# Conformer convolution: TensorE blocks in three of eight chunks, VectorE on two chunks in turn, the stage in one written order

## The chip, the core and the metric

The kernel runs on one core of a Trainium2 chip. A core has five engines that take their own instruction streams and wait for each other by semaphores: TensorE (PE in the profile, with its weight loads as PEld), VectorE (DVE), ScalarE (ACT), GpSimd (POOL) and SyncE (SP), which here only starts transfers. Matrix products go to PSUM, everything else lies in SBUF. The metric is the device time of one execution in microseconds; the time before is the median of three runs.

## The reference

A two-layer decoder trunk over 512 tokens with 1024 channels. Layer 0 has a recurrent and pooling mixer, layer 1 a conformer convolution; each layer goes on with cross-attention into 256 memory tokens and a gated MLP. The change lies in the conformer of layer 1:

```python
def conformer_conv(x, norm, w1, b1, dw_w, dw_b, ln_g, ln_b, w2, b2):
    h = rms_norm(x, norm) @ w1 + b1
    h = jax.nn.glu(h, axis=-1)
    h = causal_dwconv(h, dw_w, dw_b)
    h = jax.nn.silu(layer_norm(h, ln_g, ln_b))
    return h @ w2 + b2
```

`causal_dwconv` gives each of 1024 channels its own 31 taps over time: output t is the sum over s of tap s times the input at t - s, plus a bias. The cross-attention that follows needs keys and values of the memory, which do not depend on x: `k = (m @ wk)`, `v = (m @ wv)`.

## The kernel before

Activations lie as 8 chunks of 128 channels by 512 tokens, channels on the partitions. Every float32 operand of a product is split into a high part (rounded, written by ScalarE) and a low part (the difference, written by VectorE or GpSimd), and a product is three products, high-high, high-low and low-high: `mm3`, lines 183 to 185. A 1024 x 128 weight is one transfer into a `raw` buffer (three of them), split into `whi` and `wlo` (four of each).

The conformer is the function `conformer`, line 1342. Its steps for chunk c:

- Norm: `Scaled.scale` takes token sums on TensorE (L316), their root and reciprocal on ScalarE and VectorE (L323, L324), a diagonal (L326), and spreads it to all partitions on TensorE (L256). `split` scales x (L265) and makes its high (L173) and low half (L178).
- Projections: a gate half and a value half, `project` or `project_all`, each 24 products into a PSUM buffer named `mm`.
- Gating: ScalarE's sigmoid (L1349), then VectorE's `h = (value + bias) * sigmoid` (L1362).
- Convolution, three ways at once. *TensorE*: `conv_pe` (L1391) takes the first `4 * PE_GROUPS[c]` taps. Four transfers first make a stacked copy of h with four shifts (L1369), `spread` (L1381, GpSimd) lays taps on small diagonals, and a group of four taps is four 128 x 32 products. *ScalarE and GpSimd*: five taps, scaled copies (L1410, L1413) added up by GpSimd (L1414). *VectorE*: all others, one SCALAR_TENSOR_TENSOR a shift onto the PSUM accumulator (L1416).
- `merge` (L1425): accumulator plus bias plus GpSimd's sum. After chunks 3 and 7, `quarters` (L293) adds four chunks into the LayerNorm mean.

Before, TensorE takes 3, 2, 3, 2, 3, 3, 3 and 8 groups of the eight chunks. Chunk 7 leaves nothing to VectorE. The order of the main part is the scheduler's, from the order of the program and priorities; only the last part, from chunk 7's block on, is in written order for TensorE, ScalarE, VectorE and GpSimd (`tc.manual_schedule`). SyncE's order is the scheduler's throughout. Keys 0 to 3 of layer 1's attention (`mem.keys`, 24 products of 256 columns each) stand ahead of the norm's use, keys 4 to 7 further down. The value sums (`mem.sums`, L442) fill TensorE while the LayerNorm's chain runs.

Of the kernel before, what the change touches and what calls it, by code (L numbers as in the profile page):

```python
# [15 lines left out]
P = 128  # L16
T = 512
# [18 lines left out]
PE_GROUPS = [3, 2, 3, 2, 3, 3, 3, 8]  # L36
N_POOL = [5] * 7 + [0]
LAG = 5

KE = 4  # L40
# [6 lines left out]
    ("c_dw_w", (TAPS - 4 * min(PE_GROUPS)) * C), ("c_dw_b", C), ("c_ln_g", C), ("c_ln_b", C), ("c_b_pw2", C),  # L47
# [12 lines left out]
def trunk(ctx: ExitStack, tc: tile.TileContext, I: dict, out: list):  # L60
# [32 lines left out]
    def tmp_f(n=T):  # L93
        return tmp.tile([P, n], F32, tag="tmp", name=nm("tmp"))
# [139 lines left out]
    class Scaled:  # L234


        def __init__(self, gain):
            self.gain, self.x, self.ss = gain, [None] * C, None

        def feed(self, c):  # L240
            sq = tmp_f()
            A.activation(sq, X[c], AF.Square)
# [26 lines left out]
        def high(self, c):  # L269
            self.x[c] = self.x[c], high(self.x[c])  # L270
# [18 lines left out]
    def quarters(ps, xs):  # L289

        def quarter(j):
            n = len(xs) - 4 + j
            return PE.matmul(ps[32 * j : 32 * j + 32], onesf[:, :32], xs[n], start=n < 4, stop=n >= 4)  # L293


        with tc.issue_after(quarter(3).ins):
            for j in range(3):
                quarter(j)
# [500 lines left out]
    def ffn(layer, norm, nxt, seven):  # L799
# [267 lines left out]
        if nxt:  # L1067
            mem = Memory(1)
            mem.operand(0)
            mem.operand(1)  # L1070
            mem.outputs()
            parked = []
            for n in range(KE):
# [268 lines left out]
    def conformer(norm, nxt, mem, parked):  # L1342
# [4 lines left out]
        def gate(c, psb):  # L1347
            b = tmp_f()
            A.activation(b, psb, AF.Sigmoid, bias=col("c_b_pw1", C + c))  # L1349
            return b  # L1350

        def pieces(c):
            return load_w(I["pw1"][C + c], V if c == 2 else G), load_w(I["pw1"][c], G)

        def glu(c, w):
            b = gate(c, project(w[0], c, norm.x))
            gated(c, b, project(w[1], c, norm.x))

        def gated(c, b, psa):
            h = tmp.tile([P, T + 4], F32, tag="h", name=nm("h"), bufs=4)  # L1360
            G.memset(h[:, :4], 0.0)
            V.scalar_tensor_tensor(h[:, 4:], psa, col("c_b_pw1", c), b, op0=ALU.add, op1=ALU.mult)  # L1362
            stacked = [act_f() for _ in range(4)]
            for j in range(4):
# [5 lines left out]
            hs[c] = h[:, 4:], stacked  # L1370

# [13 lines left out]
        def conv_pe(c):  # L1385

            accs[c] = aux_ps()
# [7 lines left out]


            with tc.issue_after(tile(0, 3).ins):
                for g in range(PE_GROUPS[c]):
                    for j in range(3 if g == 0 else 4):
                        last = tile(g, j)  # L1400
            return last

        def conv(c):
            h, ps = hs[c][0], accs[c]
            z = act_f()
            first = 4 * PE_GROUPS[c]
            for s in range(first, first + N_POOL[c]):
                if s == first:
# [6 lines left out]
            for i, s in enumerate(range(first + N_POOL[c], TAPS)):  # L1415
                V.scalar_tensor_tensor(ps[:, s:], h[:, : T - s], tap(s, c), ps[:, s:], op0=ALU.mult, op1=ALU.add)  # L1416
                if i == LAG and pend:
                    merge(*pend.pop())
            if pend:
                merge(*pend.pop())  # L1420
            pend.append((c, z, ps))

        def merge(c, z, ps):
            if N_POOL[c]:
                V.scalar_tensor_tensor(z, ps, col("c_dw_b", c), z, op0=ALU.add, op1=ALU.add)  # L1425
            else:
                A.activation(z, ps, AF.Identity, bias=col("c_dw_b", c))
            outs.append(z)
            if c % 4 == 3:
                quarters(mu, outs)  # L1430

        pend, taps = [], [None] * C
        accs = [None] * C
        w = [load_w(I["pw1"][n]) for n in (C, 0, C + 1, 1)]
# [5 lines left out]
        spread(0)  # L1440
        spread(1)
        with tc.high_priority(URGENT):
            for c in range(C):
                norm.split(c)
        ps = project_all(w[:3], norm.x)
        gated(0, gate(0, ps[0]), ps[1])
        gated(1, gate(1, ps[2]), project(w[3], 1, norm.x))
        mu = stat_ps()
        w = pieces(2)
        for c in range(C - 1):  # L1450
            b = None
            if c == 0:
                b = gate(2, project(w[0], 2, norm.x))
            if c == 1:
                gated(2, gate2, project(w[1], 2, norm.x))
                w = pieces(3)
            elif c > 1:
                glu(c + 1, w)
                if c < C - 2:
                    w = pieces(c + 2)  # L1460
            gate2 = b
            if c in (0, C - 2):
                mem.keys(KE + c // 6)
            conv_pe(c)
            if c < C - 2:
                spread(c + 2)
            conv(c)
        xs = [None] * C
        with tc.manual_schedule(engines=ORDERED):
            w = [mem.key_piece(n) for n in (KE + 2, KE + 3)]  # L1470
            mem.eng = G
            ready = [mem.piece(i, park=True) for i in range(3)]
            for n in range(2):
                mem.keys(KE + 2 + n, w[n])
            ready.append(mem.piece(3, park=True))
            last = conv_pe(C - 1)
            ps = [[mm_ps(), mm_ps()] for _ in range(2)]
            z = act_f()
            A.activation(z, accs[C - 1], AF.Identity, bias=col("c_dw_b", C - 1))
            merge(*pend.pop())  # L1480
            outs.append(z)
            mem.eng = None
            ready += [mem.piece(i) for i in (4, 5)]
# [7 lines left out]
            quarters(mu, outs)  # L1491
# [6 lines left out]
            for c in range(C):  # L1498
# [3 lines left out]
                if c == 3:  # L1502
                    go(3)
                    quarters(var, sqs)
# [3 lines left out]
            quarters(var, sqs)  # L1508
# [214 lines left out]
def _layout(inputs):  # L1723
# [3 lines left out]
    a["c_dw_w"] = a["c_dw_w"][:, : TAPS - 4 * min(PE_GROUPS)]  # L1727
# [51 lines left out]
```

## Time and profile before

| | |
|---|---|
| runs | 1446.60, 1447.25, 1445.86 us; median 1446.6 |
| the profiled execution | 1445.47 us, of which the span is 1443.0 us |
| granted TensorE clock | 0.999 |
| TensorE busy | 1433.5 us, 99% of the span |
| VectorE, ScalarE, GpSimd busy | 81%, 55%, 19% |
| the stretch 774 to 871 us (convolution) | TensorE 97.0 of 97.0 us, VectorE 85.0, ScalarE 41.4, GpSimd 72.6 |

Times in the trace count from the start of the span. A row of the timeline has start, length, engine, line, operation and, in brackets, the idle time ahead of it and what ended that. TensorE's instructions are pipelined: the distance between starts says more than a length. In rows of groups, the count is behind the x, then busy time and mean ns of one, then idle time ahead. An instruction's line is that of the kernel it belongs to.

### The profile page before, as it was taken

Reading aid. Unit: us, or ns where it says so; the run is one execution under the profiler, and the core shown is the slowest. Engines: PE = TensorE matmul, PEld = TensorE weight load, DVE = VectorE, ACT = ScalarE, POOL = GpSimd, SP = SyncE. Lnnn points to the kernel's source line nnn. Section 1 sums busy time; section 2 is a strip of 40 time slices with the busy share of each in tenths; the row PEclk is TensorE's granted clock in tenths of the full one; section 3 lists DMA queues with packets and bytes.
Section 4 is the critical chain, followed back from the end, with each engine's and each line's share of the span. In section 5 each row is a group of like instructions: output and inputs, shape, how many; then the busy total and the mean of one; then the engine's idle time right before and its main releaser. Section 6 shows DMA issues by size and latency. Waiting matters only on the chain.

```text
span 1443.0 us, 22827 instructions
## 1 busy us (share of the span) xinstructions
PE 1433.5 (99%) x8608; PEld 1260.1 (87%) x8608; DVE 1162.5 (81%) x1916; ACT 787.3 (55%) x1305; POOL 274.8 (19%) x307
## 2 busy tenths in 40 slices
PE   9999999999999999999999999999999999999997
PEld 8888888988899999999887676899888999999997
DVE  6987775768788888888875897878788888888885
ACT  7668754657544444444545447666664444444433
POOL 0012300100022212212006841010001222221201
PEclk9999999999999999999999999999999999999999
DMA  8522232532567777876526654335245777777741
GB/s 303 190 88 89 89 130 73 125 96 88 161 151 166 185 157 166 181 168 146 158 88 177 165 155 151 112 81 138 90 124 128 173 183 159 168 182 163 160 126 59
DMA packets 80398, 205.33 MB, mean 142 GB/s; under 512 B 8992, under 2 KB 10272, under 8 KB 80288
## 3 DMA queue, kind: packets, MB, share of 16 engines
q1 hardware_dynamic: 53504, 155.36, 34.6%
q0 software_dynamic: 26496, 48.25, 20.4%
q8 instruction: 67, 1.10, 0.3%
q14 instruction: 43, 0.35, 0.1%
q10 hardware_dynamic: 288, 0.27, 0.1%
HBM read 145.13 MB, written 2.10 MB: 102 GB/s over the span
## 4 chain that ended last, share of the span: by engine, by line
PE 95%; DVE 2%; ACT 1%; DMA 1%; issue 0%; POOL 0%; SPq 0%; DVEq 0%; POOLq 0%; ACTq 0%
PE mm L183 23%; PE mm L184 23%; PE mm L185 23%; PE aux L183 7%; PE aux L184 7%; PE aux L185 7%; PE mm L442 3%; PE aux L1391 2%; PE aux L515 0%; DMA raw<-in_wv 0%; DVE wlo L164 0%; POOL tmp L1234 0%; DMA raw<-in_wdown 0%; ACT whi L163 0%; PE stat L316 0%
## 5 line engine op out<-in xcount | busy, mean ns | idle before, releaser
L183 PE MATMUL mm<-act,whi 128*128 128x512 f32 (+2 forms) x1093 | 385.3, 354 | 0.3 <-ACT act L849 0.3
L184 PE MATMUL mm<-act,whi 128*128 128x512 f32 (+2 forms) x1093 | 385.0, 352 | 0.1
L185 PE MATMUL mm<-act,wlo 128*128 128x512 f32 (+2 forms) x1093 | 384.7, 352 | 0.0
L183 PEld LDWEIGHTS mm<-act,whi 128*128 128x128 f32 x1093 | 206.3, 189 | 35.1 <-issue 3.3
L184 PEld LDWEIGHTS mm<-act,whi 128*128 128x128 f32 x1093 | 206.6, 189 | 29.4 <-DVE act L164 1.0
L185 PEld LDWEIGHTS mm<-act,wlo 128*128 128x128 f32 x1093 | 206.6, 189 | 27.1
L779 ACT ACTIVATE bigr<-raw 128x512 fp32r<-128x512 f32 x160 | 100.5, 629 | 158.5 <-DMA raw<-wa 67.8
L185 PE MATMUL mm<-bigr,bigr 128*128 128x256 f32 x640 | 181.1, 283 | 0.0
L184 PE MATMUL mm<-bigr,bigr 128*128 128x256 f32 x640 | 181.1, 283 | 0.0
L183 PE MATMUL mm<-bigr,bigr 128*128 128x256 f32 x640 | 180.9, 283 | 0.0
L168 DVE TENSOR_TENSOR tmp<-mm,tmp 128x256 f32<-128x256 f32 x322 | 130.9, 419 | 34.1 <-PE mm L185 27.8
L183 PE MATMUL aux<-act,whi 128*128 128x512 f32 x399 | 156.3, 392 | 0.0
L184 PE MATMUL aux<-act,whi 128*128 128x512 f32 x399 | 156.2, 392 | 0.0
L185 PE MATMUL aux<-act,wlo 128*128 128x512 f32 x399 | 155.2, 389 | 0.0
L163 ACT ACTIVATE whi<-raw 128x1024 fp32r<-128x1024 f32 (+1 forms) x95 | 96.2, 1019 | 96.7 <-PE mm L184 64.7
L786 DVE TENSOR_TENSOR bigr<-raw,bigr 128x512 fp32r<-128x512 f32 x160 | 109.9, 688 | 33.3 <-ACT bigr L779 31.2
L164 DVE TENSOR_TENSOR wlo<-raw,whi 128x1024 fp32r<-128x1024 f32 (+1 forms) x84 | 103.0, 1230 | 31.5 <-ACT whi L163 31.4
L184 PEld LDWEIGHTS mm<-bigr,bigr 128*128 128x128 f32 x640 | 122.7, 192 | 1.6
L183 PEld LDWEIGHTS mm<-bigr,bigr 128*128 128x128 f32 x640 | 122.7, 192 | 1.6
L185 PEld LDWEIGHTS mm<-bigr,bigr 128*128 128x128 f32 x640 | 122.7, 192 | 0.0
L789 POOL DMA_DIRECT2D raw<-raw x46 | 39.8, 866 | 359.3 <-DVE wlo L786 316.0
L793 POOL DMA_DIRECT2D raw<-wa x46 | 39.7, 864 | 302.4 <-DVE bigr L786 252.5
(338 smaller groups left out, 2958.4 us busy)
## 6 DMA issues: line engine op xcount, KB each, us to landing
raw<-wa POOLq DMA_DIRECT2D x138, 256.0 KB, 4.5
big<-in_wdown SPq DMA_DIRECT2D x42, 512.0 KB, 6.7
wa<-in_wpair SPq DMA_DIRECT2D x80, 256.0 KB, 3.4
raw<-in_wpair SPq DMA_DIRECT2D x40, 512.0 KB, 5.7
raw<-in_pw SPq DMA_DIRECT2D x24, 512.0 KB, 3.5
raw<-raw POOLq DMA_DIRECT2D x46, 256.0 KB, 7.5
raw<-in_win SPq DMA_DIRECT2D x20, 512.0 KB, 3.3
raw<-in_wk SPq DMA_DIRECT2D x16, 512.0 KB, 4.2
```

Source lines behind the costliest of these rows:

```text
L163: A.activation(hi, src, AF.Copy)
L164: fetched[1] = (eng or V).tensor_tensor(lo, src, hi.bitcast(F32), op=ALU.subtract)
L168: V.tensor_tensor(out, a, b, op=ALU.add)
L183: PE.matmul(ps, wh, xh, start=first, stop=False)
L184: PE.matmul(ps, wh, xl, start=False, stop=False)
L185: PE.matmul(ps, wl, xh, start=False, stop=last)
L442: PE.matmul(p, m[j], x, start=k == 0 and j == 0 and x is hi, stop=k == C - 1 and x is lo)
L779: A.activation(self.w[name][0], self.block(name), AF.Copy)
L786: V.tensor_tensor(lo, self.block(name), hi.bitcast(F32), op=ALU.subtract)
L789: G.dma_start(self.r, self.z, accum_op=ALU.add)
L793: G.dma_start(self.r, self.a22, accum_op=ALU.add)
L1391: return PE.matmul(accs[c][32 * j : 32 * j + 32, s:], taps[c][:, 4 * g + j], hs[c][1][j][:, : T - s], start=s == 0, stop=g == PE_GROUPS[c] ...
```

## The change

`PE_GROUPS` becomes 0, 0, 0, 6, 0, 5, 0, 6: TensorE blocks only in chunks 3, 5 and 7, 17 groups in place of 27. Their accumulators come from the `mm` buffers. A chunk without a block makes no stacked copies (12 transfers remain of 32); its accumulator starts with a TENSOR_SCALAR for shift 0 on VectorE, and ScalarE and GpSimd take shifts 1 to 5. All eight chunks now have five taps there. VectorE's shifts go from 106 to 140.

The whole stage from the first projections on is one written order for TensorE, ScalarE, VectorE, GpSimd and now SyncE. It is given as a script of short steps: G and V a gate and value projection, F the next load and the split of the next weight (with GpSimd for the low half), g and S sigmoid and gating, T shifts on VectorE, P taps on ScalarE and GpSimd, C a TensorE block, W its taps, M merge, K, k, l a key's products, high and low half, Q the LayerNorm sums. Steps T of two chunks stand in turn. Only keys 0 and 1 stay ahead of the norm (`KE` = 2; four keys' weights are still split ahead, `PARKED`). The norm's chunks are written as scaled(c + 1) ahead of low(c), and two one-element activations (`warm`) take ScalarE's table loads earlier: `token` (square root) and `gates` (sigmoid). The parameter block holds 31 taps a channel in place of 23.

TensorE at the norm, before. The last products of key 1, the spread, then key 2 (`mm_7771`):

```order
L183 MATMUL mm_7732<-bigr_7468,act_7514 128x256
L184 MATMUL mm_7732<-bigr_7469,act_7514 128x256
L185 MATMUL mm_7732<-bigr_7468,act_7515 128x256
L256 MATMUL aux_7769<-tmp_7767,unit 128x512
L183 MATMUL mm_7771<-bigr_7458,act_7526 128x256
L184 MATMUL mm_7771<-bigr_7459,act_7526 128x256
```

The same place now (lines are one or two higher; `mm_7738` is key 1, `mm_7832` the first gate projection):

```order
L184 MATMUL mm_7738<-bigr_7468,act_7514 128x256
L257 MATMUL aux_7775<-tmp_7773,unit 128x512
L185 MATMUL mm_7738<-bigr_7469,act_7514 128x256
```
```order
L184 MATMUL mm_7738<-bigr_7468,act_7514 128x256
L185 MATMUL mm_7738<-bigr_7469,act_7514 128x256
L186 MATMUL mm_7738<-bigr_7468,act_7515 128x256
L184 MATMUL mm_7832<-act_7781,whi_7683 128x512
L185 MATMUL mm_7832<-act_7785,whi_7683 128x512
```

The spread moves up into the middle of key 1, and the first projection follows key 1 at once.

VectorE's shifts at the first chunks, before (`aux_8076` and `aux_8168` are the accumulators of chunks 0 and 1, `h_8145` is chunk 2's gating):

```order
L1416 SCALAR_TENSOR_TENSOR aux_8076<-h_7954,par,aux_8076 128x490
L1416 SCALAR_TENSOR_TENSOR aux_8076<-h_7954,par,aux_8076 128x489
L1362 SCALAR_TENSOR_TENSOR h_8145<-mm_8120,par,tmp_8041 128x512
L1416 SCALAR_TENSOR_TENSOR aux_8076<-h_7954,par,aux_8076 128x488
L1416 SCALAR_TENSOR_TENSOR aux_8076<-h_7954,par,aux_8076 128x487
L1416 SCALAR_TENSOR_TENSOR aux_8168<-h_7992,par,aux_8168 128x499
L1416 SCALAR_TENSOR_TENSOR aux_8076<-h_7954,par,aux_8076 128x486
```

And now, where chunk 1 opens beside chunk 0 (`aux_7918` chunk 0, `aux_8054` chunk 1, `bigr_7479` the low half of key 3):

```order
L1423 SCALAR_TENSOR_TENSOR aux_7918<-h_7916,par,aux_7918 128x491
L1359 SCALAR_TENSOR_TENSOR h_8048<-mm_7983,par,tmp_7965 128x512
L1423 SCALAR_TENSOR_TENSOR aux_7918<-h_7916,par,aux_7918 128x490
L1425 TENSOR_SCALAR aux_8054<-h_8048,par 128x512
L1423 SCALAR_TENSOR_TENSOR aux_7918<-h_7916,par,aux_7918 128x489
L1423 SCALAR_TENSOR_TENSOR aux_8054<-h_8048,par,aux_8054 128x506
L179 TENSOR_TENSOR bigr_7479<-mm_8016,bigr_7478 128x256
L1423 SCALAR_TENSOR_TENSOR aux_7918<-h_7916,par,aux_7918 128x488
```

Seventeen shifts of chunk 0 now come ahead of chunk 1's gating; from there two accumulators take turns.

VectorE at the end of the stage, before: the last shifts of chunk 6 (`aux_8793`), its merge, and the low halves of three weights:

```order
L1416 SCALAR_TENSOR_TENSOR aux_8793<-h_8629,par,aux_8793 128x482
L1425 SCALAR_TENSOR_TENSOR actf_8806<-aux_8793,par,actf_8806 128x512
L164 TENSOR_TENSOR wlo_8987<-raw_8984,whi_8986 128x1024
L164 TENSOR_TENSOR wlo_8993<-raw_8990,whi_8992 128x1024
L164 TENSOR_TENSOR wlo_9017<-raw_9014,whi_9016 128x1024
```

And now (`actf_8584` is chunk 6's result, `mm_8879` chunk 7's accumulator, `bigr_7481` the low half of key 7):

```order
L1429 SCALAR_TENSOR_TENSOR actf_8584<-aux_8587,par,actf_8584 128x512
L1423 SCALAR_TENSOR_TENSOR mm_8879<-h_8711,par,mm_8879 128x483
L1423 SCALAR_TENSOR_TENSOR mm_8879<-h_8711,par,mm_8879 128x482
L1429 SCALAR_TENSOR_TENSOR actf_8723<-mm_8879,par,actf_8723 128x512
L179 TENSOR_TENSOR bigr_7481<-mm_8921,bigr_7480 128x256
L165 TENSOR_TENSOR wlo_8977<-raw_8974,whi_8976 128x1024
```

The last merge, which the LayerNorm sums wait for, stands behind two shifts of chunk 7, and two of the three weights' low halves have gone to GpSimd.

The diff, cut to its core:

```diff
-PE_GROUPS = [3, 2, 3, 2, 3, 3, 3, 8]
-N_POOL = [5] * 7 + [0]
-LAG = 5
-KE = 4
+PE_GROUPS = [0, 0, 0, 6, 0, 5, 0, 6]
+N_POOL = 5
+KE = 2
+PARKED = 4
+READY = 6
...
         def high(self, c):
-            self.x[c] = self.x[c], high(self.x[c])
+            hi = act_r()
+            self.copied.append(A.activation(hi, self.x[c], AF.Copy).ins)
+            self.x[c] = self.x[c], hi
...
         def conv_pe(c):
-            accs[c] = aux_ps()
+            accs[c] = mm_ps()
...
+        def shifts(c):
+            ss = list(range(4 * PE_GROUPS[c], TAPS))
+            at = 0 if PE_GROUPS[c] else 1
+            return ss[at : at + N_POOL], ss[:at] + ss[at + N_POOL :]
...
+        def conv(c):
+            h, (_, own) = hs[c][0], shifts(c)
+            ps = accs[c] = accs[c] or aux_ps()
+            for s in own:
+                if s:
+                    V.scalar_tensor_tensor(ps[:, s:], h[:, : T - s], tap(s, c), ps[:, s:], op0=ALU.mult, op1=ALU.add)
+                else:
+                    V.tensor_scalar(ps, h, tap(s, c), None, op0=ALU.mult)
+                yield
+
+        def merge(c):
+            V.scalar_tensor_tensor(zs[c], accs[c], col("c_dw_b", c), zs[c], op0=ALU.add, op1=ALU.add)
+            outs.append(zs[c])
+
+        def warm(name, func, ins):
+            with tc.issue_after(ins):
+                A.activation(small.tile([P, 1], F32, tag="warm", name=name, bufs=1), eps, func)
...
+        def fetch():
+            if len(raws) < len(names):
+                k, n = names[len(raws)][0], int(names[len(raws)][1:])
+                src = I["pw1"][n + (C if k == "G" else 0)] if k in "GV" else I["wk" if k == "K" else "wv"][mem.layer * C + n]
+                raws.append(wp.tile([P, D], F32, tag="raw", name=nm("raw"), bufs=3))
+                Memory.fetched = nc.sync.dma_start(raws[-1], src)
...
+        warm("token", AF.Sqrt, norm.square)
         for n in range(KE):
             mem.keys(n, parked[n])
...
+        with tc.high_priority(URGENT), tc.manual_schedule(engines={mybir.EngineType.Activation, mybir.EngineType.DVE}):
+            norm.scaled(0)
             for c in range(C):
-                norm.split(c)
+                norm.high(c)
+                if c + 1 < C:
+                    norm.scaled(c + 1)
+                norm.low(c)
+        warm("gates", AF.Sigmoid, norm.copied[3])
...
+        with tc.manual_schedule(engines=ORDERED | {mybir.EngineType.SP}):
+            ps0 = project_all([ws["G0"], ws["V0"]], norm.x)
...
+            run("G1 F S0 T0 F T0 P0 T0 P0 T0 P0 T02 K2 g1 T0 F T0 P0 T0 P0 T0 V1 k2 l2 T06 K3 F T0 S1 T0 P1 T1 P1 T0")
...
+            run("F T65 K7 M6 T72 M7 k7 l7")
...
-            quarters(mu, outs)
+            quarters(mu, outs, 1)
```

More of the change, by code (lines that the diff above doesn't have):

```diff
@@ L1072, in ffn @@
             parked = []
-            for n in range(KE):
+            for n in range(PARKED):
                 if n + 1 < C // 2:
@@ L1345, in conformer, with sigmoid, gated @@
         hs, outs = [None] * C, []
[L1347 to L1359, printed above, removed]
[L1360 to L1364 removed]
+        b, psa = [None] * C, [None] * C
+        def sigmoid(c, psb):
+            b[c] = tmp_f()
+            A.activation(b[c], psb, AF.Sigmoid, bias=col("c_b_pw1", C + c))
+        def gated(c):
+            h = tmp.tile([P, T + 4], F32, tag="h", name=nm("h"), bufs=4)
+            if PE_GROUPS[c]:
+                G.memset(h[:, :4], 0.0)
+            V.scalar_tensor_tensor(h[:, 4:], psa[c], col("c_b_pw1", c), b[c], op0=ALU.add, op1=ALU.mult)
+            stacked = []
+            for j in range(4 if PE_GROUPS[c] else 0):
+                stacked.append(act_f())
                 v = h[32 * j : 32 * j + 32, 1 : 1 + T].unsqueeze(1).broadcast_to([32, 4, T])
@@ L1394, in tile, with set_aside @@
                 )
[L1397 to L1408, printed above, removed]
+            for g in range(PE_GROUPS[c]):
+                for j in (3, 0, 1, 2) if g == 0 else range(4):
+                    tile(g, j)
+        def shifts(c):
+            ss = list(range(4 * PE_GROUPS[c], TAPS))
+            at = 0 if PE_GROUPS[c] else 1
+            return ss[at : at + N_POOL], ss[:at] + ss[at + N_POOL :]
+        def set_aside(c):
+            h, (pool, _) = hs[c][0], shifts(c)
+            z = zs[c] = act_f()
+            for s in pool:
+                if s == pool[0]:
                     G.memset(z[:, :s], 0.0)
@@ L1435, in conformer @@
+        for _ in range(4):
+            fetch()
+            weights()
+        fetch()
+        fetch()
+        warm("token", AF.Sqrt, norm.square)
         for n in range(KE):
@@ L1450, in conformer @@
[L1450 to L1467, printed above, removed]
```

115 lines of the change are left out of this document (65 added, 50 removed).

## The prediction

> **What bounds the kernel now.** I read the page's head first, then the busy times of the stage that the change rewrites, then the chain of waits there, then the timelines of VectorE and ScalarE.
>
> ```profile
> span 1443.0 us, 22827 instructions
> PE 1433.5 (99%) x8608; PEld 1260.1 (87%) x8608; DVE 1162.5 (81%) x1916; ACT 787.3 (55%) x1305; POOL 274.8 (19%) x307
> ```
>
> TensorE is busy for 99% of the span, so a microsecond of TensorE work counts unless something opens a gap. The busy times from the token sums of the conformer's norm to the first product of the value sums, and on to the next stage, say the same:
>
> ```profile
> 735.58:870.59 135.01, 135.01 (x780) 1.00 0.51 142
> 870.59:899.00 28.41, 28.41 (x135) 1.00 0.48 158
> ```
>
> Columns: length, TensorE busy (instructions), granted clock, DMA share, GB/s. There is no idle TensorE in either stretch; the clock is full. The chain of waits in order of time shows what the convolution's blocks take in it:
>
> ```profile
> 775.28 2.69 PE aux L1391 x24
> 777.98 0.43 PE mm L183
> 778.40 0.23 PE mm L184
> ...
> 783.65 1.85 PE aux L1391 x16
> ...
> 863.78 6.82 PE aux L1391 x64
> 870.60 2.99 PE mm L442 x12
> 873.59 1.00 PE stat L293 x8
> ```
>
> A block of 3 groups of taps is 24 instructions in 2.69 us, one of 2 groups 1.85, one of 8 groups 6.82. The product behind a block takes 0.43 where its neighbours take 0.23. The last row is the second half of the LayerNorm sums, which needs all eight chunks.
>
> **TensorE, removed.** Before: five blocks of 3 groups, two of 2, one of 8: 5 x 2.69 + 2 x 1.85 + 6.82 = 23.97, and 8 x 0.20 for the product behind each: 25.6 us. After: blocks of 6, 5 and 6 groups. From 3 to 8 groups the price rises by (6.82 - 2.69) / 5 = 0.826 a group, so 5.17 + 4.34 + 5.17, and 3 x 0.20: 15.3 us. **TensorE does 10.3 us less**, all of it on the path if nothing opens. Projections, keys and value sums are only moved.
>
> **TensorE, opened: the norm.** Keys 2 and 3 no longer stand between the norm and the first projection. What they cover now:
>
> ```profile
> 734.67 1.05 PE L316 MATMUL stat<-onesf,tmp 128*128 128x1 f32 x8
> 735.58 0.36 PE L184 MATMUL mm<-bigr,act 128*128 128x256 f32 x1
> ...
> 738.42 1.02 PE L256 MATMUL aux<-tmp,unit 128*128 128x512 f32 x2
> ...
> 739.51 0.28 PE L185 MATMUL mm<-bigr,act 128*128 128x256 f32 x1
> 739.63 0.28 PE L183 MATMUL mm<-bigr,act 128*128 128x256 f32 x1
> ```
> ```profile
> 735.15 1.28 ACT L323 ACT_TABLE_LOAD   x1
> 736.44 0.26 ACT L323 ACTIVATE rtok<-stat,eps 128x4 f32<-128x4 f32 x1
> ...
> 740.26 0.63 ACT L173 ACTIVATE act<-actf 128x512 fp32r<-128x512 f32 x1 [1.26 <-DVE actf L265]
> ```
> ```profile
> 736.74 0.18 DVE L324 RECIPROCAL rtok<-rtok 128x4 f32<-128x4 f32 x1 [1.15 <-ACT rtok L323]
> 736.95 0.69 DVE L326 TENSOR_TENSOR tmp<-ident,rtok 128x512 f32<-128x512 f32 x1
> 739.48 0.75 DVE L265 SCALAR_TENSOR_TENSOR actf<-x,par,aux 128x512 f32<-128x512 f32 x1
> 740.92 0.69 DVE L178 TENSOR_TENSOR act<-actf,act 128x512 fp32r<-128x512 f32 x1 [0.70 <-ACT act L173]
> 741.53 0.74 DVE L265 SCALAR_TENSOR_TENSOR actf<-x,par,aux 128x512 f32<-128x512 f32 x1
> ```
>
> The sums end at 735.6. The square root then waits for a table load that the new `token` row takes earlier, so it starts near 735.75 and the scale is ready at 736.95, not 737.64. Key products are 0.12 us apart, so 12 of them put `spread` at 737.05 and its end at 738.0. VectorE's first scaled chunk (0.75) ends at 738.8, its high half (0.63) at 739.45; the other 11 key products end at 739.3. TensorE waits 0.2, runs one product, and waits 0.45 for the low half (0.69, done at 740.15). From then on VectorE needs 0.66 + 0.62 = 1.28 us a chunk, because high and low no longer follow each other (now 741.53 - 739.48 = 2.05), and TensorE 6 x 0.227 = 1.36: no further wait. **Cost 0.7 us**; the first two projections end at 751.0. Bounds: 0, and what today's pace of 2.05 would open in eight chunks, 8 x 0.69 = 5.5. I take 0.7, since each step is a row.
>
> **VectorE, added.** Shifts go from 106 to 140. Their pitch depends on the neighbour. The seven from 864.58 all go to one accumulator; the 13 from 826.26 change accumulator each time:
>
> ```profile
> 783.68 0.75 DVE L1362 SCALAR_TENSOR_TENSOR h<-mm,par,tmp 128x512 f32<-128x512 f32 x1 [0.22 <-PE mm L185]
> 784.35 8.48 DVE L1416 SCALAR_TENSOR_TENSOR aux<-h,par,aux 128x488 f32<-128x488 f32 x13
> ...
> 826.26 8.34 DVE L1416 SCALAR_TENSOR_TENSOR aux<-h,par,aux 128x495 f32<-128x495 f32 x13 [0.57 <-PE aux L1391]
> 834.51 0.74 DVE L1425 SCALAR_TENSOR_TENSOR actf<-aux,par,actf 128x512 f32<-128x512 f32 x1
> ...
> 861.40 0.42 DVE L164 TENSOR_TENSOR bigr<-mm,bigr 128x256 fp32r<-128x256 f32 x1
> 861.73 2.26 DVE L1416 SCALAR_TENSOR_TENSOR aux<-h,par,aux 128x491 f32<-128x491 f32 x3
> ...
> 864.58 5.30 DVE L1416 SCALAR_TENSOR_TENSOR aux<-h,par,aux 128x488 f32<-128x488 f32 x7
> ```
>
> One shift lasts about 0.73, so the pitch is (5.30 - 0.73) / 6 = 0.762 on one accumulator and (8.34 - 0.73) / 12 = 0.634 between two. In the new order 108 follow another accumulator (or another operation), 27 their own, and 5 are the new first shift (TENSOR_SCALAR from SBUF into PSUM), which the trace lacks. Its nearest rows are
>
> ```profile
> L1249 DVE TENSOR_SCALAR tmp<-mm,par 128x512 f32<-128x512 f32 x2 | 1.6, 800 | 0.0
> L1162 DVE TENSOR_SCALAR big<-big,smt 128x512 f32<-128x512 f32 x1 | 0.5, 489 | 0.1
> ```
>
> one with PSUM as source, one without PSUM: 0.49 to 0.80, I take 0.6, the middle, since it has one operand in each; the ends move the sum by 1 us. Gating and merging are 0.66 apart (784.35 - 783.68), a key's low half 0.33. Sum from the first gating to the last merge: 108 x 0.634 + 27 x 0.762 + 5 x 0.6 + 16 x 0.66 + 5 x 0.33 = 104.3. Laid along the order beside TensorE's row sums, gating waits for the value projection in five chunks, 0.7 to 0.9 each, and two key lows wait 1.3 together: 5.6 with the small ones. The 15.2 of other work (5 x 0.6 + 16 x 0.66 + 5 x 0.33) return below. Start: 751.0 plus the sigmoid, 751.8. **Last merge: 861.7.** TensorE reaches the value sums at 870.6 - 10.3 + 0.7 = 861.0, and after 12 products (2.99) the LayerNorm sums at 864.0. VectorE is 2.3 us early: **0 us**. A slower VectorE loses its 5.6 us of waits first, so the cover ends where 751.8 + 15.2 + 135 pitches reach 863.8 (0.2 for the handover): at a mean pitch of 0.717, where the sum above has 0.66.
>
> **GpSimd and ScalarE, added.** GpSimd's prices:
>
> ```profile
> L164 POOL TENSOR_TENSOR wlo<-raw,whi 128x1024 fp32r<-128x1024 f32 x11 | 26.6, 2416 | 68.4 <-ACT whi L163 68.4
> L164 POOL TENSOR_TENSOR act<-raw,act 128x512 fp32r<-128x512 f32 x8 | 10.1, 1308 | 0.0
> ...
> L1414 POOL TENSOR_TENSOR actf<-actf,tmp 128x496 f32<-128x496 f32 x5 | 6.3, 1269 | 0.2
> ```
>
> 18 x 2.42 + 8 x 1.31 + 32 x 1.27 = 94.7, with about 5 for the taps 100 us between 752.7 and 862: nearly full, so it matters who waits for it. Weights arrive over 10 us ahead of their projection along the order; the last low half is ready at 862 and used in the second value sums near 878. Hidden; at 10 to 14% slower the last merge would come 1 us later, still hidden. ScalarE does 5 more copies for the eighth chunk and stays half idle.
>
> **SyncE, moved.** 20 stacked copies go. One of the attention's loads now stands ahead of three weight loads and waits for chunk 4's last shift, near 841; those loads wait for their own buffers until 850 anyway: 0. The longer parameter load, 33 KB at the very start, is one transfer among many: 0 to 0.4 us, taken as 0.
>
> **Sum.** -10.3 + 0.7 = -9.6. Behind the stage TensorE is never idle and its order is the same, so the gain stays. The profiled execution took 1445.5 (span 1443.0 and 2.5 around it) and would take 1435.9; the median of the runs, 1446.6, is 1.1 above it: **1437.0 us**.
>
> **Rivals.**
> *VectorE is late.* If alternating brings nothing, all 135 shifts cost 0.762, the waits vanish, and the last merge is 751.8 + 15.2 + 102.9 = 869.9; the LayerNorm sums start at 870.1, 6.1 us late: 1443.1. For it: VectorE has 8% to spare, after which each us counts. Against: the 13 shifts at 826.26. A part of this, a mean pitch of 0.73 to 0.76, gives 1438.8 to 1443. Chance 0.16 together.
> [...]
> *VectorE decides: slower.* Same place, a higher price. The sign turns when the last merge is at 873.6, a pitch of 0.79. At 0.83 it is 751.8 + 15.2 + 112.1 = 879.1, 15.3 us late: 1452.3. For it: the PSUM-source row of 0.80 among VectorE's operations of this size. Against: none of the 106 shifts has such a pitch. Chance 0.08.
> *The norm opens more.* If the table load or the halves' order does not help as above, 0.7 becomes 1.5 to 5.5; at 3.2 the time is 1439.5. For it: eight short handovers among three engines. Chance 0.10.
> *Something unnamed*, slower: 0.04.
>
> **How the numbers follow.** The forecast has 0.62, within 1435.6 (no gap at the norm, less the runs' scatter of 0.7) and 1438.8 (2 us late). The range adds late VectorE and the norm: 1435.6 to 1443.5. Within 0.2%, 2.9 us, a measurement of this kernel tells nothing: 1443.7 to 1449.5. Faster: 0.62 + 0.14 + 0.10 = 0.86. Same: 0.02 + 0.02 + 0.01 = 0.05. Slower: 0.06 + 0.03 = 0.09.
>
> **What would show it.** TensorE busy near 125.4 us from the token sums to the value sums, idle below 1 us, almost all at the first projection. VectorE's last merge 2 us ahead of the LayerNorm sums, pitch 0.63 where two chunks are open. The prediction is wrong if TensorE waits at the second LayerNorm sums, at the last key (it needs the PSUM buffer of chunk 5's merge) or at a block for its stacked copies.

## The result: 1446.5 us before, 1436.1 after

| | before | after |
|---|---|---|
| median of six runs | 1446.53 us (1445.86 to 1447.25) | 1436.11 us (1435.68 to 1437.28) |
| profiled execution | 1445.47, span 1443.0 | 1436.11, span 1434.3 |
| ratio | | 0.9929, 95% interval 0.9916 to 0.9942 |

The change is faster by 0.7%, some 10 us; forecast were 1437.0 us and a gain of 9.6. The page's head after it:

```profile
span 1434.3 us, 22661 instructions
PE 1424.3 (99%) x8528; PEld 1258.6 (88%) x8528; DVE 1174.0 (82%) x1944; ACT 791.1 (55%) x1311; POOL 291.7 (20%) x309
```

TensorE has 80 instructions less and is still busy for 99%; VectorE has gained 28 instructions. The busy times of TensorE, over the same two stretches as before (from the product behind the token sums to the first product of the value sums, and on):

```profile
736.82:862.16 125.34, 124.91 (x700) 1.00 0.39 116
862.16:890.00 27.84, 27.84 (x133) 1.00 0.42 132
```

The stage is 125.34 us long where it was 135.0, and TensorE has 0.43 idle in it where it had none. The waits of TensorE in it name both:

```profile
PE mm L185 <- DVE act L179: 0.2, 1, 0.2
PE mm L184 <- ACT act L272: 0.2, 1, 0.2
```

Columns: line waiting and line waited for, us, times, longest. These are the first products on the norm's first high and low half. VectorE's timeline in the middle and at the end of the stage, with TensorE's second LayerNorm sums behind it:

```profile
752.72 0.75 DVE L1359 SCALAR_TENSOR_TENSOR h<-mm,par,tmp 128x512 f32<-128x512 f32 x1 [2.49 <-ACT tmp L1353]
753.50 0.75 DVE L1425 TENSOR_SCALAR aux<-h,par 128x512 f32<-128x512 f32 x1
754.29 6.99 DVE L1423 SCALAR_TENSOR_TENSOR aux<-h,par,aux 128x506 f32<-128x506 f32 x9
...
780.27 0.75 DVE L1359 SCALAR_TENSOR_TENSOR h<-mm,par,tmp 128x512 f32<-128x512 f32 x1 [0.69 <-PE mm L186]
780.94 0.74 DVE L1429 SCALAR_TENSOR_TENSOR actf<-aux,par,actf 128x512 f32<-128x512 f32 x1
781.72 0.75 DVE L1425 TENSOR_SCALAR aux<-h,par 128x512 f32<-128x512 f32 x1
782.38 8.46 DVE L1423 SCALAR_TENSOR_TENSOR aux<-h,par,aux 128x498 f32<-128x498 f32 x13
...
857.22 0.42 DVE L179 TENSOR_TENSOR bigr<-mm,bigr 128x256 fp32r<-128x256 f32 x1 [1.83 <-ACT bigr L174]
857.56 3.77 DVE L1423 SCALAR_TENSOR_TENSOR aux<-h,par,aux 128x486 f32<-128x486 f32 x5
861.43 0.75 DVE L1429 SCALAR_TENSOR_TENSOR actf<-aux,par,actf 128x512 f32<-128x512 f32 x1
862.10 1.48 DVE L1423 SCALAR_TENSOR_TENSOR mm<-h,par,mm 128x483 f32<-128x483 f32 x2
863.68 0.75 DVE L1429 SCALAR_TENSOR_TENSOR actf<-mm,par,actf 128x512 f32<-128x512 f32 x1
```
```profile
865.00 1.06 PE L296 MATMUL stat<-actf,onesf 128*32 128x512 f32 x8
```

The nine shifts at 754.29, one behind the other in chunk 0, have a pitch of (6.99 - 0.72) / 8 = 0.78; the 13 at 782.38, in turn between two accumulators, (8.46 - 0.72) / 12 = 0.645. The last merge ends at 864.43, 0.6 us before the sums start. So the chain of events is the forecast one, with a margin of 0.6 where 2.3 were forecast.

### The profile page after: what moved, and what is told of

It is laid out like the page before. It is cut to its first block, busy times and chain, and to the rows that moved or that the text cites. A ratio compares the mean times of both kernels' runs of the same rounds, so it can differ in the third digit from the quotient of the medians.

```text
span 1434.3 us, 22661 instructions
## 1 busy us (share of the span) xinstructions
PE 1424.3 (99%) x8528; PEld 1258.6 (88%) x8528; DVE 1174.0 (82%) x1944; ACT 791.1 (55%) x1311; POOL 291.7 (20%) x309
## 4 chain that ended last, share of the span: by engine, by line
PE 94%; DVE 2%; DMA 1%; ACT 1%; issue 0%; POOL 0%; SPq 0%; DVEq 0%; ACTq 0%; POOLq 0%
PE mm L185 23%; PE mm L184 23%; PE mm L186 23%; PE aux L184 7%; PE aux L185 7%; PE aux L186 7%; PE mm L444 2%; PE mm L1389 1%; DMA raw<-in_wv 1%; DVE wlo L165 1%; PE aux L517 0%; DMA raw<-in_wk 0%; ACT whi L164 0%; POOL tmp L1236 0%; PE stat L318 0%
## 5 line engine op out<-in xcount | busy, mean ns | idle before, releaser
L788 DVE TENSOR_TENSOR bigr<-raw,bigr 128x512 fp32r<-128x512 f32 x160 | 109.9, 687 | 32.2 <-ACT bigr L781 29.9
L165 DVE TENSOR_TENSOR wlo<-raw,whi 128x1024 fp32r<-128x1024 f32 (+1 forms) x77 | 92.9, 1209 | 26.7 <-ACT whi L164 26.6
```

The costliest lines, as they stand in the source:

```text
L165: fetched[1] = (eng or V).tensor_tensor(lo, src, hi.bitcast(F32), op=ALU.subtract)
L788: V.tensor_tensor(lo, self.block(name), hi.bitcast(F32), op=ALU.subtract)
```

## The experiments

The stage lengths in this section run from the token sums' first product to the value sums' first, start to start: 735.90 to 862.16 in the changed kernel, **126.26 us**, and 734.67 to 870.53, 135.86, in the kernel before. Two executions of the changed kernel agree in them within 0.02 us, while medians of four or five runs are uncertain by about 2 us (0.13%).

| run | what it does | median, us | ratio to before, interval | stage, us |
|---|---|---|---|---|
| the changed kernel | | 1436.11 | 0.9929 (0.9916 to 0.9942) | 126.26 |
| e13_after_again | the same | 1436.80 | 0.9933 (0.9918 to 0.9948) | 126.24 |
| e1_blocked | little alternation (33 of 140 shifts) | 1441.53 | 0.9964 (0.9951 to 0.9977) | 127.48 |
| e2_norm_seq | halves one after the other | 1440.24 | 0.9959 (0.9944 to 0.9974) | 131.05 |
| e3_no_warm | table loads not ahead | 1436.88 | 0.9936 (0.9921 to 0.9951) | 127.49 |
| e7_ke4 | keys 2, 3 ahead of the norm | 1435.15 | 0.9919 (0.9902 to 0.9935) | 125.20 |
| e12_two_acc | that, and chunk 0 on two accumulators | 1433.62 | 0.9916 (0.9900 to 0.9933) | 125.19 |
| e8_c5_six | one group more on TensorE | 1435.93 | 0.9927 (0.9912 to 0.9942) | 127.05 |
| e9_c7_five | one group less | 1439.89 | 0.9949 (0.9932 to 0.9966) | 125.40 |
| e10_late_keys | one less, keys late | 1460.69 | 1.0097 (1.0082 to 1.0112) | 151.41 |
| e11_old_order | fewer groups in the old order | 1452.00 | 1.0039 (1.0024 to 1.0054) | 141.83 |

In e1 and e9 the wait lies behind the first value sums, so outside this stretch.

**Is alternation worth anything?** e1_blocked sorts the steps T of the script by chunk, between two steps S, M, l or C:

```diff
-... T2 P2 T1 T2 P2 T1 V3 F T2 T1 g3 T2 T1 T2 T1 T2 T1 G4 F S3 ...
+... T1 P2 T1 T1 P2 T1 V3 F T1 T1 g3 T2 T2 T2 T2 T2 T2 G4 F S3 ...
```

> The shifts on VectorE are the same 140, but within each stretch between two gatings, merges or key lows they stand chunk by chunk instead of in turn: 33 follow another accumulator or another operation and 107 their own, where the changed kernel has 113 and 27. Theory (the pitch depends on whether the accumulator changes): with the changed kernel's own rows, 0.64 in turn and 0.78 on one accumulator, VectorE needs 80 x 0.14 = 11 us more; its 4.6 us of waits are used up first and its margin of about 0.5 ahead of the second LayerNorm sums next, so TensorE waits there for 5.5 to 9 us and the time is 1441.5 to 1445. Rival (the order of the accumulators is worth nothing, and the longer rows have another cause): VectorE's length stays, TensorE does not wait at those sums, 1436 within 1.

VectorE's timeline and TensorE's:

```profile
781.88 5.37 DVE L1423 SCALAR_TENSOR_TENSOR aux<-h,par,aux 128x498 f32<-128x498 f32 x7
787.16 0.75 DVE L1425 TENSOR_SCALAR aux<-h,par 128x512 f32<-128x512 f32 x1
787.94 4.66 DVE L1423 SCALAR_TENSOR_TENSOR aux<-h,par,aux 128x506 f32<-128x506 f32 x6
```
```profile
868.71 1.93 PE L296 MATMUL stat<-actf,onesf 128*32 128x512 f32 x8 [3.22 <-DVE actf L1429]
870.58 2.93 PE L444 MATMUL mm<-act,bigr 128*128 128x512 f32 x6
```

The same shifts now stand 0.775 apart, (5.37 - 0.72) / 6, and TensorE waits at the second LayerNorm sums, as the theory said. The wait is 3.2 us, less than the 5.5 expected, and another 1.1 lies ahead at chunk 7's block, for its stacked copies: VectorE's gating of that chunk stands 110.3 us behind the token sums (845.43), where it stood 104.2 (840.11). But the eight sums then take 1.93 where they took 1.06, and the six products 2.93 where they took 1.66: the granted clock is 0.50 from 868.70 to 874.20, behind the wait, which e9_c7_five below shows more closely. The median is 5.4 us slower, so the alternation, with the slow clock behind that wait, is worth about half of the change's gain of 10.4.

**The accumulator or the source?** When chunks alternate, both change. e12_two_acc keeps one source: in the kernel with keys 2 and 3 ahead (below), the first 18 shifts of chunk 0 go in turn to two accumulators, added to chunk 0's result by a new step J.

```diff
+            if c == 0:
+                both[:] = [ps, aux_ps()]
-            for s in own:
+            for i, s in enumerate(own):
+                if c == 0:
+                    ps = both[i % 2 if i < 18 else 0]
...
+                    elif k == "J":
+                        V.tensor_tensor(zs[0][:, 6:], zs[0][:, 6:], both[1][:, 6:], op=ALU.add)
```

> The kernel with keys 2 and 3 ahead of the norm, and one thing more: the first 18 shifts of chunk 0, which stand alone on VectorE, alternate between two accumulators, and the second is added to the chunk's result by one more operation on VectorE. The source, h, stays the same for all 18. Theory (it is the accumulator, written by one shift and read by the next, that sets the pitch): the 16 pitches fall from 0.78 to 0.64, 2.3 us less for 0.66 more, and the last merge stands 2.3 to 2.6 us ahead of the second LayerNorm sums in place of 0.9; the time stays near 1435.2, since TensorE did not wait. Rival (in alternation it is the change of source that helps): the pitch stays at 0.78, and the last merge comes 0.7 later, 0.2 ahead of the sums.

Chunk 0's shifts without the edit (e7_ke4), then with it, both from VectorE's timeline, and the last rows with it:

```profile
759.19 12.40 DVE L1423 SCALAR_TENSOR_TENSOR aux<-h,par,aux 128x506 f32<-128x506 f32 x16
```
```profile
758.24 9.75 DVE L1429 SCALAR_TENSOR_TENSOR aux<-h,par,aux 128x505 f32<-128x505 f32 x15
...
854.49 0.42 DVE L179 TENSOR_TENSOR bigr<-mm,bigr 128x256 fp32r<-128x256 f32 x1 [0.86 <-ACT bigr L174]
854.83 3.77 DVE L1429 SCALAR_TENSOR_TENSOR aux<-h,par,aux 128x486 f32<-128x486 f32 x5
...
860.96 0.75 DVE L1435 SCALAR_TENSOR_TENSOR actf<-mm,par,actf 128x512 f32<-128x512 f32 x1
```

(12.40 - 0.72) / 15 = 0.779 became (9.75 - 0.73) / 14 = 0.644, with the source unchanged. So here it is the accumulator: a shift that reads what the one before it wrote starts 0.135 us later. Two accumulators are also two PSUM buffers, so this run alone could mean that the same buffer twice in a row costs more. But the step shows in SBUF too, in the changed kernel's rows above: the first shift of chunk 0, which reads the `h` that the gating has just written, starts 0.78 behind it (752.72 to 753.50), while a merge of another chunk starts 0.67 behind a gating (780.27 to 780.94). The second half of the expectation failed: the last merge ends at 861.71, 0.9 ahead of the sums at 862.62, as without the edit. What VectorE gained it spent waiting: 0.3 at step J and 0.86 at key 6's low half. Behind that low half, which follows TensorE's key 6 and ScalarE's copy of it, stand 7.2 us of VectorE's work (854.49 to 861.71; 857.22 to 864.43 in the changed kernel). The margin at the LayerNorm sums hangs on this tail; work saved ahead of it did not widen it.

**One group up, one group down.** e8_c5_six gives chunk 5's block a sixth group and takes four of its shifts from VectorE; e9_c7_five does the opposite in chunk 7.

```diff
-PE_GROUPS = [0, 0, 0, 6, 0, 5, 0, 6]
+PE_GROUPS = [0, 0, 0, 6, 0, 6, 0, 6]    (e8: six steps T5 become two)
+PE_GROUPS = [0, 0, 0, 6, 0, 5, 0, 5]    (e9: "M6 T72 M7" becomes "M6 T76 M7")
```

> Chunk 5's block gets 6 groups in place of 5, and VectorE loses four of that chunk's six shifts. Theory (TensorE's own work sets the time, one group costs 0.83 us): the stretch from token sums to value sums is 0.8 longer, VectorE's last merge stands 2.5 to 3.5 us ahead of the LayerNorm sums, in place of 0.5, and the time is 1436.9. Rival (VectorE sets it): VectorE has 2.5 us less to do, and the time is 1435.5 or less.

> The opposite step: chunk 7's block gets 5 groups in place of 6, and VectorE makes four more of its shifts, which stand one behind the other at the very end. Theory (the margin at the second LayerNorm sums is 0.5 us): the four cost 4 x 0.78 = 3.1 on one accumulator, TensorE arrives 0.83 earlier, and waits there for 3.1 + 0.8 - 0.5 + 0.1 = 3.5; the sum is 2.7 slower, 1438.8. Rival (VectorE still has the 2.3 us that the prediction gave it): a wait of 1.6, 0.8 slower, 1436.9. If VectorE were free altogether, 0.83 faster, 1435.3.

For e8 the stage is 0.8 us longer (127.05), as one group's price says; the median, 1435.93, cannot tell this from nothing. The margin at the sums grew only to 1.1 us, because VectorE now waits 3.7 us for two key copies in place of 1.8 for one. For e9 TensorE's timeline and its busy times around the sums:

```profile
867.20 1.93 PE L296 MATMUL stat<-actf,onesf 128*32 128x512 f32 x8 [3.63 <-DVE actf L1429]
```
```profile
863.50:867.20 3.70, 0.07 (x2) 0.01 (x1) 3.49 (x6) 0.00 (x0) 0.00 (x0) 0.79 0.68 220
867.20:870.90 3.70, 3.70 (x12) 1.69 (x13) 0.34 (x2) 1.54 (x2) 0.00 (x0) 0.50 0.30 85
870.90:872.60 1.70, 1.70 (x6) 1.03 (x4) 1.16 (x1) 0.00 (x0) 0.00 (x0) 0.53 0.04 10
```

The wait is 3.6, where 3.5 was expected: the margin is 0.6, not 2.3. But the sum, 2.7, came out as 3.8 in the medians, and in the trace, from the token sums to the 18 products behind the mean (735.90 to 867.95, and 735.25 to 872.59), as 5.3. The granted clock (first number behind the five engines) shows why: it is 0.50 and 0.53 in the 5.4 us behind the wait, and 1.00 again from 872.60 to 877.20. The same sums and products take 2.4 us longer (867.20 to 872.59, for 865.00 to 867.95 in the changed kernel). The mean of 0.79 over 3.70 us puts the fall from 1.00 to 0.50, if it was a single step, 1.55 us ahead of the sums, 2.1 us into the wait: an estimate. In e1_blocked the clock is 0.90 on average from 865.40 to 868.70 and 0.50 from there to 874.20, which by the same estimate puts the fall 0.66 us ahead of 868.70, some 2.5 us into the wait. Executions of one kernel differ in this: e9's four runs go from 1437.67 us (mean granted clock 0.998) to 1440.77 (0.996), e1's five from 1439.75 (0.999) to 1442.74 (0.997), and the profiled one is the longest in both. So, in this order, the split of the taps lies at its balance: a group less on VectorE's side gains nothing that can be measured and costs 0.8 us of TensorE, a group more costs several us.

**The norm.** e2_norm_seq writes each chunk as scaled, high, low again; e3_no_warm leaves out the two early table loads.

```diff
-            norm.scaled(0)
             for c in range(C):
+                norm.scaled(c)
                 norm.high(c)
-                if c + 1 < C:
-                    norm.scaled(c + 1)
                 norm.low(c)
```

> The norm's chunks are written scaled, high, low one after the other again, on ScalarE and VectorE, and nothing else changes. Theory (VectorE, in order, waits for ScalarE's high half before it may scale the next chunk): a chunk costs VectorE 2.05 us, as in the kernel before, where TensorE needs 1.36 for its six products; TensorE waits 7 x 0.69 = 4.8 more at the first two projections, and all behind it is as much later: 1441. Rival (the halves' order is worth nothing, because the two engines overlap anyway): TensorE's idle time at the norm stays at 0.4, 1436.

TensorE's timeline shows one chunk's step, from low half to low half:

```profile
740.56 0.50 PE L185 MATMUL mm<-act,whi 128*128 128x512 f32 x1 [0.23 <-DVE act L179]
740.89 0.39 PE L186 MATMUL mm<-act,wlo 128*128 128x512 f32 x1
741.13 0.39 PE L184 MATMUL mm<-act,whi 128*128 128x512 f32 x1
741.36 0.40 PE L185 MATMUL mm<-act,whi 128*128 128x512 f32 x1
741.59 0.39 PE L186 MATMUL mm<-act,wlo 128*128 128x512 f32 x1
741.88 0.51 PE L184 MATMUL mm<-act,whi 128*128 128x512 f32 x1
742.61 0.50 PE L185 MATMUL mm<-act,whi 128*128 128x512 f32 x1 [0.22 <-DVE act L179]
```

The step is 2.05, the stage 4.8 longer, both as expected, and the time 4.1. The listed wait is only 0.22 a chunk, though each chunk loses 0.69: the product that waited, and the one ahead of it, are shown longer (0.50 for 0.39) and their starts further apart. So here the listed idle time is too small, and the starts tell the price.

```diff
-        warm("token", AF.Sqrt, norm.square)
...
-        warm("gates", AF.Sigmoid, norm.copied[3])
```

> The two one-element activations that take the table loads earlier are left out. Key 0's high half then stands ahead of the load for the square root. Theory: a load starts as soon as ScalarE has done the instruction before it, without waiting for the operand of its own; so the one for the square root begins when key 0's copy ends, near 736.3 in the changed kernel's time, and the square root comes 0.6 to 0.7 us later, which TensorE waits at the first projection; the one for the sigmoid fits into ScalarE's idle time of 2.5 us ahead of the first sigmoid and costs nothing: 1436.7. Rival: a load waits for its activation's operand: then the sigmoid, VectorE's first gating and its last merge come 1.3 later too, beyond its margin of 0.5, and the time is 1437.5.

ScalarE's timeline:

```profile
734.55 0.38 ACT L164 ACTIVATE bigr<-mm 128x256 fp32r<-128x256 f32 x1 [1.46 <-PE mm L186]
734.96 1.28 ACT L325 ACT_TABLE_LOAD   x1
736.25 0.26 ACT L325 ACTIVATE rtok<-stat,eps 128x4 f32<-128x4 f32 x1
...
749.12 1.28 ACT L1353 ACT_TABLE_LOAD   x1
751.78 0.69 ACT L1353 ACTIVATE tmp<-mm,par 128x512 f32<-128x512 f32 x1 [1.37 <-PE mm L186]
```

Both loads start within 0.03 us of the end of ScalarE's instruction before (734.93 and 749.10), without waiting for their activation's operand; the one for the sigmoid is hidden, with 1.4 us to spare, as expected. The square root comes 1.77 behind the start of the token sums, where it came 1.09: 0.7 later, as expected. The stage grew by 1.2, though: in this kernel's order the spread stands behind all of key 1's products, where the changed kernel has 11 of them (1.3 us) behind it, and so TensorE had nothing to do while the first chunk was scaled. So `token` is worth 0.7 by itself and up to 1.2 with the place of the spread that came with it; `gates` is worth nothing here.

**Do the two keys serve better behind the norm or ahead of it?** e7_ke4 moves keys 2 and 3 ahead again (`KE` = 4, without steps K2, k2, l2, K3, k3, l3).

> Keys 2 and 3 stand ahead of the norm's first projection again, out of the written order, and nothing else changes. Theory (VectorE sets the end of this stage, and the two keys behind the projections are its cover): TensorE's 0.4 us of idle time at the norm goes, but VectorE's first gating comes 48 x 0.12 - 0.4 = 5.3 us later against TensorE's own end; its waits for the value projections (2.0) vanish, its margin of 0.5 too, and TensorE waits 1 to 3 us at the second LayerNorm sums: 1437 to 1439. Rival (TensorE alone sets the end; VectorE has room): the gap of 0.4 is gone and nothing opens, 1435.7.

The rival was right. The stage is 125.20, 1.06 shorter, no wait of TensorE is listed in it, and VectorE is in time by 0.9 us, though it starts 5 us later:

```profile
757.61 0.75 DVE L1359 SCALAR_TENSOR_TENSOR h<-mm,par,tmp 128x512 f32<-128x512 f32 x1 [6.41 <-ACT tmp L1353]
...
856.04 0.42 DVE L179 TENSOR_TENSOR bigr<-mm,bigr 128x256 fp32r<-128x256 f32 x1
856.37 3.77 DVE L1423 SCALAR_TENSOR_TENSOR aux<-h,par,aux 128x486 f32<-128x486 f32 x5
```

The expectation had counted 2.0 us of VectorE's waits as reserve. All 4.6 that the changed kernel has between 753 and 864 were reserve (2.0 and 0.8 for value projections, 1.8 for key 6's copy), and two key lows (0.7) left the stage. So this part of the change costs a microsecond: e7_ke4 and e12_two_acc are the best kernels here. The medians say so too (1435.15 and 1433.62), but no interval of theirs excludes the changed kernel's ratio.

**Waits turned into shifts?** e10_late_keys takes one group off chunk 7 and moves keys 2 and 3 behind the last projection.

```diff
-... V1 k2 l2 T06 K3 F T0 S1 ...
+... V1 T06 F T0 S1 ...
...
+... S7 T4 P7 T6 P7 M4 C5 K2 F P7 T6 P7 T6 T5 T6 k2 T5 K3 ...
```

> Chunk 7's block gets 5 groups, as in the run before, but the order makes room: keys 2 and 3 move behind the last projection, so that the value projections come 5.8 us earlier and VectorE's waits for them (0.7, 0.3, 0.6, 0.5, 0.8) go; its wait of 1.8 for key 6 goes too, since the key lows stand later; chunk 7's block stands ahead of keys 5 and 6, and its six shifts alternate with chunk 6's. Theory (VectorE's waits can be turned into shifts): VectorE gets 4.7 us less idle time for 2.5 of work and is on time; TensorE does 0.83 less, and may wait 0 to 0.5 at chunk 7's block for its stacked copies: 1435.3 to 1435.8. Rival (the waits come back at another place, at chunk 7's block or at the key lows): TensorE waits 1 to 3 us at the second LayerNorm sums, 1436.3 to 1438.

1460.7 us, worse than both. TensorE's waits and ScalarE's:

```profile
PE mm L1389 <- POOL big L1379: 13.0, 1, 13.0
PE mm L184 <- ACT tmp L1353: 4.8, 1, 4.8
PE mm L186 <- POOL wlo L165: 3.1, 1, 3.1
```
```profile
ACT actf L1410 <- PE mm L1389: 26.1, 1, 26.1
```

ScalarE stood for 26 us at a chunk's first tap until TensorE had done an earlier chunk's block, and GpSimd's adds and low halves, which stand behind, and TensorE's next block behind these. The tap's result, the stacked copies and the halves of keys 2 and 3 all come from one pool of 32 buffers (tag `act`), and eight of them hold these keys' weights until their products are done. The early place of the two keys frees these buffers, which neither theory had counted. That this is the cause follows from the code and from who waited for whom; no run of its own shows it.

**TensorE's part alone.** e11_old_order makes the blocks of the kernel before smaller and leaves its order.

```diff
-PE_GROUPS = [3, 2, 3, 2, 3, 3, 3, 8]
-N_POOL = [5] * 7 + [0]
+PE_GROUPS = [2, 2, 2, 2, 2, 2, 2, 6]
+N_POOL = [5] * 8
```

> The kernel before, with its own scheduled order, and only its blocks made smaller: two groups in each of the first seven chunks and six in the last, 20 groups in place of 27, and 22 shifts more on VectorE (128). Theory (less TensorE work pays only where the order gives VectorE the time for it): TensorE has 7 x 0.83 = 5.8 us less, so the second LayerNorm sums could start at 867.7; VectorE, busy for 79.5 of the 87.2 us from its first block chunk at 783.6 on, gets 22 x 0.64 = 14.1 more and has 7.7 idle, so its last merge moves from 870.7 to about 876; TensorE waits 8 us there, and runs slower for a few us after it, as in the runs where it waited over 3 us: 1449 to 1453. Rival (the work moved is hidden, whatever the order): 1440.8.

The old order has no shifts for chunk 7 at all, so this kernel leaves out that chunk's last seven taps, and VectorE has 20 shifts more, not 22. The time is 1452.0, within the theory's range: seven groups less (5.8 us) on TensorE made the kernel 6 us slower. The range was met, the place was not: TensorE waits 3.7 and 4.5 us, not at the LayerNorm sums but at the last two blocks. Both start 0.1 us behind the end of a merge (856.37 and 870.03), which by the code frees the accumulator that the block needs:

```profile
856.47 2.50 PE L1391 MATMUL aux<-actf,big 128*32 128x512 f32 x16 [3.68 <-issue]
870.13 7.51 PE L1391 MATMUL aux<-actf,big 128*32 128x512 f32 x48 [4.51 <-DVE actf L1425]
```

48 instructions take 7.51, where the changed kernel's six groups take 5.26, and 16 take 2.50, where the block at 842.79 took 1.89: the slow clock again (0.90 on average from 840 to 890 us, where the changed kernel has 1.00 in the stage and behind it).

**How much of a time is the start?** e5_before_again is the kernel before, unchanged, e13_after_again the changed one.

> The kernel before, unchanged, profiled once more. In its first profile the second group of token sums starts at 23.0 us, in the changed kernel's at 24.1, and the token sums of the conformer's norm come 1.2 us later there. Theory (the first 25 us, which wait for the first loads, differ from execution to execution): the sums at 23.0 come between 23.2 and 25 this time, the span is longer than 1443.0 by as much, and the stretch from the conformer's token sums to the value sums is 135.0 again. Rival (the start of the changed kernel is slower because of its change): 23.0 and 1443.0 come again within 0.2.

> The changed kernel once more, beside the two above. Theory (the first 25 us differ from execution to execution, the rest does not): 126.3 from the conformer's token sums to the first value sum again, an idle 0.4 at the norm, the last merge 0.5 ahead of the LayerNorm sums; the time between 1435 and 1437. Rival (the fast stage is one execution's luck): one of these differs by over 0.5.

The second group of token sums starts at 23.0 us in the first profile of the kernel before and at 24.1 in that of the changed kernel. e5 gave 23.0 and a span of 1442.9 again, as the rival said. But its neighbours of the same kernel had spans from 1443.3 to 1445.9, e11, with the short parameter block too, had 24.2, and the ten profiles of the changed kernel and its variants 23.2 to 24.9. So the start scatters by 1.7 us among those ten, and whether the change has a part in it stays open. e13 gave the stage again within 0.02, the waits, and a margin of 0.4.

## Right and wrong, step by step

- **TensorE removed, -10.3.** Right. Without the gap at the norm (e7_ke4) the stage is 135.86 - 125.20 = 10.66 shorter; one group more (e8) cost 0.79 for a forecast 0.83. The 0.4 over the forecast is about the step into a block, which the forecast left out: 0.32 us from the last product to the block's first (783.26 to 783.58 in the kernel before) where products stand 0.23 apart, so 0.09 for each of the five blocks that are gone.
- **TensorE opened at the norm, 0.7.** Right in place, low in size. The two waits stand where they were forecast, listed as 0.2 each for 0.2 and 0.45. By starts they are 0.36 and 0.50 (products at 740.40, 740.88 and 741.61, where 0.12 and 0.23 are usual), and against e7_ke4 the norm costs 1.06 in all; the last 0.2 have no row of their own. This and the 0.4 too little above cancel, which is luck: the stage changed by 9.60, forecast 9.6. The step that kept the cost small, the halves' order, is shown by e2 (4.8); the earlier table load moves the square root by 0.68 (1.77 - 1.09, e3) for the 0.69 forecast.
- **VectorE, 0 us.** Right in sign and cause, and nearer to the edge than forecast. Start 752.7, at 753.0 when the forecast is moved by the 1.24 us that the token sums came later; end 864.43 for 862.9. The pitches were 0.645 and 0.78 for 0.634 and 0.762, the new first shift lasts 0.75 where 0.6 was taken, 0.66 to 0.79 apart. The waits were 4.6 for 5.6, but they stood elsewhere: 1.8 of them at key 6's copy, with 7.2 us of work behind it, where the forecast had 1.3 for two keys. The margin was 0.6 for 2.3: this is the term that was mis-sized, by 1.8 us of VectorE's length (111.7 for 109.9), made of the pitches, the new first shift and small gaps, although the waits were 1.0 less. The cover by mean pitch, "at 0.717", held better, since waits do vanish: e1's pitches, without the five first shifts, have a mean of (28 x 0.64 + 107 x 0.775) / 135 = 0.747, which the forecast's formula puts 4.0 us late, and the second LayerNorm sums stand 4.5 us later behind the token sums than in the changed kernel (TensorE waited 1.1 at chunk 7's block and 3.2 at the sums).
- **The rival "VectorE is late", 1443.1.** It did not come true; e1_blocked, which takes most of the alternation away, comes near it with 1441.5. The rival's price had a longer wait in it (6.1 for 3.2 and 1.1) and no slow clock. It gave every shift one pitch, 0.762; the runs show two, 0.779 on one accumulator (e7) and 0.644 between two (e12).
- **GpSimd, SyncE, ScalarE, 0.** Right: GpSimd was busy for 96.0 of the 125.3 us (about 100 forecast), and TensorE waited for none of the three in the stage beyond the first high half.
- **The sum.** The profiled spans differ by 8.7: 9.6 in the stage and 0.3 behind it, less 1.2 that the start took longer in this execution. The first profile of before had 2.5 us around its span, which the forecast used; all later runs, of both kernels, have 1.8. The median came 0.9 below the forecast, and the medians are 10.4 apart for 9.6: both within the scatter of such runs.

## What to carry to other kernels

Shifts chained on one accumulator stood 0.779 us apart (e7), a fifth more than the 0.644 of two chains in turn (e12); where two are open, write them in turn. When work is moved from a saturated engine to one with room, look for the last point at which the receiving engine is tied to the giving one, and count what stands behind it there; the slack ahead of that point hardly helped here (the margin was 0.6 in the changed kernel and 1.1 in e8, 0.9 in both e7 and e12). And price a possible wait of TensorE with the slow clock that came with the waits of 3.2 us (e1) and 3.6 (e9): 2.4 us in e9's profiled execution, the longest of its four.

## What the runs showed of the hardware

- The granted clock around a wait: in e1, with 3.2 us idle, it was 0.50 for the 5.5 us behind the wait that were measured (868.70 to 874.20); in e9, with 3.6 idle, 0.50 and 0.53 for 5.4 us behind it (867.20 to 872.60), then 1.00. By the estimate above the fall came some 2.5 and 2.1 us into the wait. In e11, behind a wait of 3.7, key products stood 0.21 us apart from 859.28 to 860.77 and 0.12 again from 861.15 on, and behind one of 4.5 six groups took 7.51 us for 5.26. The changed kernel's two waits of 0.2 at the norm left the clock at 1.00; behind e2's eight and the 1.5 in e3 products stood 0.23 to 0.24 apart, as behind those two, and behind the 1.1 in e1 six groups took 5.26. Between 1.5 and 3.1 us no run has a wait listed in the stage, and why the clock falls was not shown, so how short a wait still does it stays open.
- A shift that reads the accumulator of the one before it started 0.78 us behind it, between two accumulators 0.64 (e7 and e12, source unchanged).
- A table load on ScalarE (1.28 us) did not wait for the operand of its activation (e3: it starts at 749.12, 2.66 us ahead of the sigmoid that it is for).
